# A two-layer decoder trunk on one core: 17 expert weight slots instead of 15, the first step's pieces given back in pairs, and the final norm ahead of the overflow block

## The chip, the cores and the metric

The kernel runs on one core of a Trainium2 chip. The metric is the device time of one execution in microseconds (us). A core has TensorE (PE, with its weight loads as PEld), VectorE (DVE), ScalarE (ACT), GpSimd (POOL) and SyncE (SP); a letter q behind an engine's name means its instruction queue. SP issues all the large weight transfers, one after the other in program order.

## The reference, cut to what matters

Two layers on 256 rows of 1024 numbers, all float32. The first layer ends in a dense SwiGLU, the second in a choice of two of eight experts per row; the last part, from which most of the time comes, is this:

```python
def moe_swiglu(x, w_router, w_gu, w_down):
    logits = jnp.einsum('bsd,de->bse', x, w_router).astype(jnp.float32)
    top_logits, top_idx = lax.top_k(logits, TOP_K)
    top_gates = jax.nn.softmax(top_logits, axis=-1)
    gates = jnp.sum(jax.nn.one_hot(top_idx, N_EXPERTS, dtype=jnp.float32) * top_gates[..., None], axis=-2)
    ...
    for e in range(N_EXPERTS):
        out = out + gates[..., e:e + 1] * swiglu(x, w_gu[e], w_down[e])
    return out

def reference(...):
    ...
            ffn = moe_swiglu(x, w_router[layer // 2], w_gu_moe[layer // 2], w_down_moe[layer // 2])
        x = layer_norm(DEEPNORM_ALPHA * x + ffn, ln2_g[layer], ln2_b[layer])
```

An expert is a SwiGLU with 2816 hidden numbers: 1024 x 5632 weights up and 2816 x 1024 down, so eight experts have 277 MB of weights, and each weight is used once.

## The kernel before, in words

**Order of the work.** Each engine follows its own list of instructions in program order; nothing is chosen at run time except by branches. Up to about 480 us the dense part runs, in which weights are split into a high and a low part (`hi`, `lo`), so that three products make up one float32 product. From then on the experts run, with the raw float32 weights.

**The stream of weights.** Class `Stream` keeps a list of weight pieces of at most 1 MiB (0.75 MiB where a chunk has six column groups), in the order in which they will be used. A piece needs a raw slot. `load` asks SP for the next pieces for as long as a slot is free; `high` and `low` split a dense piece; `done` says that a split piece is used up, and `whole` and `passed` take an expert piece raw and give its slot back. Where `passed` stands in the program, the request of the piece that takes the slot stands too, behind a wait for the products that read the old one. At most eight requests are in the air.

The raw slots of the experts are 15: three that the dense part has already (`RAW = 3`), four in the memory that the attention leaves (`RAW2 = 4`, tag `raw2`), one and one in the memory of the experts (`raw3` and `MORE = 1`, tag `raw5`), and six in the place of the split pieces, three `hi` and three `lo` (`SPLIT = 3`). The last eight of these are opened together, when the dense part's memory is closed.

**Steps.** An expert's 22 column groups (of 128) are cut into chunks of 8, 8 and 6, for the first expert 2, 8, 8 and 4. `STEPS` lists (expert, chunk). A step multiplies the up pieces of its chunk (`up`), then the down pieces of the step before (`down`). There are eight up pieces and three or four down pieces in a full step. At most 64 rows of an expert are handled there; if it has more, which a branch decides (`more_than_half`), `up_more` and `down_more` do the rows 65 to 96 as well, with the same pieces. For more than 96 rows a whole second round exists, in blocks of their own, behind a branch (L1230); here no expert has that many, and the blocks are skipped. The order of the experts 2 to 7 comes from their row counts, which the kernel works out itself: `load_counts` (L969 to L974) loads nine counts into a register on every engine, and six expert numbers on SP.

**Gathers.** Before an expert's first step its rows are gathered by products with a one-hot matrix, `gather`, eight for a batch of experts, each into a PSUM bank (tag `pb`, four banks, of which `down` holds two). `BATCHES` says which experts share one; a batch is made during the expert ahead of its first, as tasks that `some(3)` and `some(2)` spread behind each step's up and down. `turn_hot` turns the one-hots for the way back, `rows_split` splits the expert's output into `yh` and `yl`, and `scatter` adds it to the rows.

**The end.** After the last expert come its `rows_split` and `scatter`, the two branches over the overflow blocks, then the norm of the rows (statistics at L322) and six output transfers (L1242).

Of the kernel before, what the change touches and what calls it, by code (L numbers as in the profile page):

```python
# [20 lines left out]
P = 128  # L21
D = 1024
# [23 lines left out]
def trunk_kernel(ctx: ExitStack, tc: tile.TileContext, x, mem, positions, w_in_a, conv_a, w_q_b,  # L46
# [20 lines left out]
    class Stream:  # L67
# [4 lines left out]
        def __init__(self):  # L72
            self.specs, self.parts, self.raw = [], {}, {}
            self.pools, self.split_pools, self.home = [], [], {}
# [22 lines left out]
        def load(self, limit=None):  # L97
            while self.n_dma < min(len(self.specs), limit or len(self.specs)):
# [8 lines left out]
                raw = p[0].tile([P, PC], F32, name="raw", tag=p[1], bufs=p[2])  # L107
# [14 lines left out]
        def high(self):  # L122
# [4 lines left out]
            hi = p[0].tile([P, PC], F32R, name="hi", tag="hi" + p[1], bufs=p[2])  # L127
# [76 lines left out]
    RAW, RAW2, MORE, SPLIT = 3, 4, 1, 3  # L204
# [125 lines left out]
    def ln_apply(dst, sl, mean, z, gb):  # L330
        nc.vector.scalar_tensor_tensor(dst[:, sl], dst[:, sl], mean, gb[:, 0, sl], op0=OP.subtract, op1=OP.mult)
        nc.vector.scalar_tensor_tensor(dst[:, sl], dst[:, sl], z, gb[:, 1, sl], op0=OP.mult, op1=OP.add)

    def ln_apply_gpsimd(dst, sl, mean, z, gb):
        nc.gpsimd.tensor_scalar(dst[:, sl], dst[:, sl], mean, z, op0=OP.subtract, op1=OP.mult)  # L335
# [512 lines left out]
    def turn_rows(tb):  # L848
        xf[tb] = early.tile([P, KT, P], F32, name="xf", tag="y", bufs=3)
# [22 lines left out]
    st.slots(ring, "hi", SPLIT)  # L872
    st.slots(ring, "lo", SPLIT)
# [15 lines left out]
    g4, e4 = [moe.tile(T4, F32, name=n, tag="sT", bufs=5) for n in ("r_g4", "r_e4")]  # L889
    cnti = moe.tile([P, 2 * NE + 1], I32, name="r_cnti")  # L890
    counts = []
# [31 lines left out]
    def first_hidden(tb, pt):  # L923
# [3 lines left out]
        hd[tb] = moe.tile([P, 2, 256], F32R, name="hd", tag="hd", bufs=2)  # L927
# [51 lines left out]
    BATCHES = ((0, 1), (2, 3, 4), (5, 6, 7))  # L979

    def experts(part):
# [24 lines left out]
        def turn_hot(e):  # L1006
# [3 lines left out]
            turned[e] = moe.tile([P, TB, P], F32R, name="sT", tag="sT", bufs=5)  # L1010
            nc.scalar.copy(turned[e][:CAP].rearrange("p t s -> p (t s)"), ps[:CAP, :TB * P])

        def batch_tasks(es):
            made = []
            return ([lambda: made.extend(one_hots(es))] + [lambda k=k: gather(*made, k) for k in range(KT)] +
                    [lambda e=e: turn_hot(e) for e in es])
# [5 lines left out]
        def up(e, c):  # L1022
# [108 lines left out]
        def first_step(gathers):  # L1131
# [17 lines left out]
            for t in gathers[1:1 + KT]:  # L1149
                t()  # L1150
# [108 lines left out]
```

## Time and profile before

| what | value |
|---|---|
| median of the runs shown | 1182.9 us (1180.91 to 1183.71) |
| the profiled execution | 1181.65 us |
| its span, first to last instruction | 1180.0 us |
| PE busy | 1082.5 us, 92% |
| DVE, ACT, POOL busy | 385.1, 257.7, 62.5 us |
| mean granted clock of PE | 0.976 |
| bytes moved | 353.85 MB |

A busy share is an average over stages with different limits; the dense part (to 480 us) and the experts' part behind it have to be read apart. The page cuts the span into 40 slices of 29.5 us.

### The profile page before, as it was taken

What the parts mean: (1) busy time and instruction counts of PE and PEld (TensorE: products, weight loads), DVE (VectorE), ACT (ScalarE), POOL (GpSimd) and SP (SyncE); (2) the same over time, 40 slices, a digit from 0 to 9 for tenths busy, and PEclk for the clock granted to TensorE, in tenths of its full rate; (3) what the DMA queues carried; (4) which work ended last, traced back from release to release, by engine and by line L of the source; (5) the groups of instructions that cost most, each with busy time, mean ns of one, the idle gap of its engine ahead of it and who ended that gap; (6) DMA issues with size and microseconds to landing.
All of it is one profiled execution on the core that took longest, in us unless ns stands there. A gap on an engine that the chain in (4) does not pass through costs nothing. (4 is left out here: it accounts for less than half of the span.)

```text
span 1180.0 us, 16954 instructions
## 1 busy us (share of the span) xinstructions
PE 1082.5 (92%) x6926; PEld 636.9 (54%) x6926; DVE 385.1 (33%) x595; ACT 257.7 (22%) x367; POOL 62.5 (5%) x47
## 2 busy tenths in 40 slices
PE   8999999999899889897888999999899999999981
PEld 7987899999787656442332343343342343343320
DVE  4767656454776557200110100110210100200105
ACT  5543443443345431110100100100110100100100
POOL 1002000000210220000000000000000000000001
PEclk9999899999989889999999999999999999999995
DMA  9647555556343226699999999999999999999982
GB/s 332 219 165 237 192 178 183 191 165 212 101 149 124 91 72 254 269 401 410 408 403 410 408 404 409 407 389 386 391 388 409 407 405 409 399 391 402 406 343 77
DMA packets 127595, 353.85 MB, mean 300 GB/s; under 512 B 6375, under 2 KB 41968, under 8 KB 127488
## 3 DMA queue, kind: packets, MB, share of 16 engines
q1 hardware_dynamic: 127392, 352.35, 78.7%
q8 instruction: 71, 1.16, 0.4%
q14 instruction: 36, 0.29, 0.1%
q0 software_dynamic: 96, 0.04, 0.0%
HBM read 351.32 MB, written 1.05 MB: 299 GB/s over the span
## 5 line engine op out<-in xcount | busy, mean ns | idle before, releaser
L65 PE MATMUL pa<-raw,xg 128*64 128x512 f32 (+4 forms) x2304 | 388.3, 556 | 21.0 <-DMA raw<-in_w_gu_moe_dram 18.0
L65 PEld LDWEIGHTS pa<-raw,xg 128*64 128x64 f32 (+1 forms) x2304 | 134.2, 128 | 263.8 <-issue 209.6
L65 PE MATMUL pb<-raw,hT 128*64 128x512 f32 x704 | 158.6, 597 | 9.4 <-DMA raw<-in_w_down_moe_dram 3.9
L128 ACT CAST hi<-raw 128x2048 fp32r<-128x2048 f32 (+2 forms) x68 | 124.7, 1836 | 138.7 <-PE pa L65 96.8
L1037 DVE TENSOR_TENSOR h<-h,pa 128x512 f32<-128x512 f32 (+2 forms) x24 | 15.3, 638 | 413.8 <-PE pa L65 401.7
L65 PE MATMUL pa<-xh,hi 128*128 128x256 f32 x528 | 149.7, 284 | 0.2 <-ACT xh L213 0.2
L65 PE MATMUL pa<-xl,hi 128*128 128x256 f32 x528 | 148.5, 281 | 0.3 <-DVE xl L214 0.3
L65 PE MATMUL pa<-xh,lo 128*128 128x256 f32 x528 | 148.5, 281 | 0.0
L138 DVE TENSOR_TENSOR lo<-raw,hi 128x2048 fp32r<-128x2048 f32 (+2 forms) x60 | 130.5, 2182 | 48.1 <-ACT hi L128 48.1
L65 PEld LDWEIGHTS pb<-raw,hT 128*64 128x64 f32 x704 | 48.5, 136 | 106.6 <-issue 88.0
L1036 ACT ACTIVATE h<-pa 128x512 f32<-128x512 f32 (+2 forms) x24 | 13.4, 557 | 416.3 <-PE pa L65 416.3
L65 PEld LDWEIGHTS pa<-xh,hi 128*128 128x128 f32 x528 | 100.0, 189 | 1.6 <-issue 0.8
L65 PEld LDWEIGHTS pa<-xl,hi 128*128 128x128 f32 x528 | 100.0, 189 | 0.9 <-DVE xl L214 0.5
L65 PEld LDWEIGHTS pa<-xh,lo 128*128 128x128 f32 x528 | 99.9, 189 | 0.1
L138 POOL TENSOR_TENSOR lo<-raw,hi 128x2048 fp32r<-128x2048 f32 x8 | 37.7, 4726 | 371.9 <-ACT hi L128 268.9
L65 PE MATMUL pb<-raw,hTx 128*32 128x256 f32 x704 | 40.3, 380 | 3.9 <-DVE hTx L1071 3.9
L1180 POOL MEMSET ya<- 32x1024 f32 x8 | 7.6, 945 | 622.3 <-DVE yl L214 611.8
L65 PE MATMUL pa<-hi,xh 128*128 128x512 f32 (+1 forms) x96 | 36.6, 381 | 0.0
L65 PEld LDWEIGHTS pb<-raw,hTx 128*32 128x32 f32 x704 | 22.5, 110 | 21.4 <-DVE hTx L1071 4.4
L65 PE MATMUL pa<-lo,xh 128*128 128x512 f32 (+1 forms) x96 | 33.9, 354 | 0.0
L1053 DVE TENSOR_TENSOR hx<-hx,pa 64x512 f32<-64x512 f32 (+1 forms) x12 | 7.8, 647 | 78.8 <-ACT hx L1052 78.8
L65 PE MATMUL pa<-hi,xl 128*128 128x512 f32 (+1 forms) x96 | 32.7, 346 | 0.0
(237 smaller groups left out, 1030.6 us busy)
## 6 DMA issues: line engine op xcount, KB each, us to landing
raw<-in_w_gu_moe_dram SPq DMA_DIRECT2D x128, 1024.0 KB, 17.9
raw<-in_w_down_moe_dram SPq DMA_DIRECT2D x88, 1024.0 KB, 17.9
raw<-in_w_gu_moe_dram SPq DMA_DIRECT2D x56, 768.0 KB, 14.7
raw<-in_w_gu_dense_dram SPq DMA_DIRECT2D x44, 512.0 KB, 4.9
raw<-in_w_down_dense_dram SPq DMA_DIRECT2D x11, 1024.0 KB, 4.9
raw<-in_w_in_a_dram SPq DMA_DIRECT2D x8, 1024.0 KB, 9.7
raw<-in_w_o_dram SPq DMA_DIRECT2D x8, 1024.0 KB, 4.9
raw<-in_w_kv_shared_dram SPq DMA_DIRECT2D x6, 1024.0 KB, 5.1
```

The source lines that it names most:

```text
L65: nc.tensor.matmul(o, l, r, start=start, stop=stop, skip_group_check=True)
L128: nc.scalar.copy(hi[:, :n], raw[:, :n])
L138: (nc.gpsimd if self.spare > 0 else nc.vector).tensor_sub(v, raw[:, :n].rearrange("p (a b) -> p a b", a=hi.shape[1]), hi)
L1036: nc.scalar.activation(h[:, :w], pg[:, :w], AF.Silu)
L1037: nc.vector.tensor_tensor(h[:, :w], h[:, :w], pu[:, :w], op=OP.mult)
L1053: nc.vector.tensor_tensor(h[64:, :w], h[64:, :w], px[64:, :w], op=OP.mult)
L1180: nc.gpsimd.memset(down.ya[HALF:CAP], 0.0)
```

## The change

It has four parts. The raw slots become 17: `raw2` has five and `raw5` two, and the six places of `hi` and `lo` are no longer opened together, but each pair when its split piece is used up for the last time (`done`, `turned`). In the first full step, (0,1), the eight up pieces are multiplied and given back in four pairs (`groups`), each with its own branch for the rows over 64. Counts are loaded one batch at a time, and only the first ahead of the first step; batches have two experts each, four batches instead of three; `rows_split` and `down_more` split straight out of PSUM into `yh` and `yl`, without the tile `ya`. The norm and the output (`finish`) stand ahead of the overflow branch, and a second time at the end of the block inside it; the second round is nested in the first, and the output goes through a tile of its own.

```diff
         def slots(self, pool, tag, bufs):
-            self.pools.append([pool, tag, bufs, 0])
+            self.pools.append([pool, tag, bufs, 0, bufs])
             return self.pools[-1]
 
         def split_slots(self, pool, tag, bufs):
             self.split_pools.append([pool, tag, bufs, 0, bufs])
+            self.turned[tag] = [[pool, t + tag, 0, 0, bufs] for t in ("hi", "lo")]
             return self.split_pools[-1]
...
         def done(self):
-            self.home.pop(self.n_done)[3] -= 1
+            p = self.home.pop(self.n_done)
+            p[3] -= 1
             self.n_done += 1
+            if p[2] and self.n_hi == self.n_split:
+
+                p[2] -= 1
+                for t in self.turned[p[1]]:
+                    if t not in self.pools:
+                        self.pools.append(t)
+                    t[2] += 1
+                self.load()
             self.pump()
...
-    RAW, RAW2, MORE, SPLIT = 3, 4, 1, 3
+    RAW, RAW2, MORE, SPLIT = 3, 5, 2, 3
...
     raw3 = st.slots(moe, "raw3", 1)
     st.slots(moe, "raw5", MORE)
-    st.slots(ring, "hi", SPLIT)
-    st.slots(ring, "lo", SPLIT)
     st.load()
...
-    def load_counts():
-        for e in [*range(NE), 2 * NE]:
-            counts.append(nc.values_load(cnti[0:1, e:e + 1], min_val=0, max_val=S))
+    def load_count(e):
+
+        if e not in counts:
+            at = e if e < NE else 2 * NE
+            counts[e] = nc.values_load(cnti[0:1, at:at + 1], min_val=0, max_val=S)
...
     acc = x3
-    BATCHES = ((0, 1), (2, 3, 4), (5, 6, 7))
...
+        def groups(e, c):
+
+            n = len(expert_up(e, c))
+            return [2] * (n // 2) if part == 0 and (e, c) == STEPS[1] else [n]
+
+        def up(e, c, n):
...
             w = CH[e][c][1] * 64
-            g, (pg, pu) = xg[e], banks(2)
-            pcs, k = [], 0
-            while k < KT:
+            if up.k == 0:
+                up.to = banks(2)
+            g, (pg, pu) = xg[e], up.to
+            pcs = []
+            for _ in range(n):
...
+            if up.k == KT:
+                up.k = 0
+                h = moe.tile([P, 512], F32, name="h", tag="h", bufs=2)
+                nc.scalar.activation(h[:, :w], pg[:, :w], AF.Silu)
+                nc.vector.tensor_tensor(h[:, :w], h[:, :w], pu[:, :w], op=OP.mult)
+                hs[e, c] = h
             return pcs
 
-        def up_more(e, c, pcs):
+        up.k = 0
...
             if c == len(CH[e]) - 1:
+                yh, yl = ys[e]
                 for q in range(4):
-                    nc.vector.tensor_copy(down.ya[HALF:CAP, 256 * q:256 * q + 256],
-                                          down.yx[32 * q:32 * q + 32, :256])
+                    sl = slice(256 * q, 256 * q + 256)
+                    split(yh[HALF:CAP, sl], yl[HALF:CAP, sl], down.yx[32 * q:32 * q + 32, :256])
...
         def rows_split(e):
-            ya = down.ya
-            yh, yl = [early.tile([P, D], F32R, name=n, tag="y", bufs=3) for n in ("yh", "yl")]
+            yh, yl = ys[e]
             for q in range(2):
-                nc.scalar.copy(ya[:HALF, 512 * q:512 * q + 512], down.y[64 * q:64 * q + 64])
-            split(yh[:CAP], yl[:CAP], ya[:CAP])
-            ys[e] = yh, yl
+                sl = slice(512 * q, 512 * q + 512)
+                split(yh[:HALF, sl], yl[:HALF, sl], down.y[64 * q:64 * q + 64])
...
+            if pc_ == len(CH[pe_]) - 1:
+                ys[pe_] = [early.tile([P, D], F32R, name=n, tag="y", bufs=2) for n in ("yh", "yl")]
+                for t in ys[pe_]:
+                    nc.gpsimd.memset(t[HALF:CAP].bitcast(F32), 0.0)
...
-            pcs = up(e, c)
-            some(3)
-            hxs[e, c] = moe.tile([P, 512], F32, name="hx", tag="hx", bufs=2)
-            if i > 0:
-                turn_both(prev, prev[0] == e, lambda: up_more(e, c, pcs))
-            else:
-                with more_than_half(e):
-                    up_more(e, c, pcs)
-            for _ in pcs:
-                st.passed()
+            (up_more.to,) = banks(1)
+            for g, n in enumerate(groups(e, c)):
+                k = up.k
+                pcs = up(e, c, n)
+                if g == 0:
+                    some(3)
+                    hxs[e, c] = moe.tile([P, 512], F32, name="hx", tag="hx", bufs=2)
+                if g == 0 and i > 0:
+                    turn_both(prev, prev[0] == e, lambda: up_more(e, c, pcs, k))
+                else:
+                    with more_than_half(e):
+                        up_more(e, c, pcs, k)
+                for _ in pcs:
+                    st.passed()
...
+    def finish():
+
+        y = moe.tile([P, TB, D], F32, name="y_out", tag="raw5", bufs=MORE)
...
+        z = ln_scale(mv, TB)
+        for tb in range(TB):
+            for f, sl in ((ln_apply_gpsimd, slice(896, D)), (ln_apply, slice(0, 448)), (ln_apply, slice(448, 896))):
+                f(y[:, tb], sl, mv[:, tb, 0:1], z[:, tb:tb + 1], gb, acc[:, tb])
+                nc.sync.dma_start(out[0, tb * P:(tb + 1) * P, sl], y[:, tb, sl])
+
     experts(0)
     st.drop(raw3)
     gb = ln_vectors(moe, ln2_g[1], ln2_b[1], tag="raw3")
-    for part in range(1, PARTS):
-        with tc.If(counts[NE] > CAP * part):
+    finish()
+
+    with tc.If(counts[NE] > CAP):
+        expert_specs()
+        st.load()
+        experts(1)
+        with tc.If(counts[NE] > 2 * CAP):
             expert_specs()
             st.load()
-            experts(part)
-
-    mv = small.tile([P, TB, 2], F32, name="ln_mv2")
-    for tb in range(TB):
-        nc.vector.bn_aggr(mv[:, tb], ln_sums(acc[:, tb], None, None))
-    z = ln_scale(mv, TB)
-    for tb in range(TB):
-        for f, sl in ((ln_apply_gpsimd, slice(896, D)), (ln_apply, slice(0, 448)), (ln_apply, slice(448, 896))):
-            f(acc[:, tb], sl, mv[:, tb, 0:1], z[:, tb:tb + 1], gb)
-            nc.sync.dma_start(out[0, tb * P:(tb + 1) * P, sl], acc[:, tb, sl])
```

Three places in the order of instructions are of interest.

The first is SP's list where the experts' stage begins, from the branch of step (0,1) on (L1169 before; L1194 and L1241 after). The DMA rows are the requests for the next pieces, where x2 or x4 counts them. Before:

```order
L1169 COMPARE_AND_BRANCH
L1169 UNCONDITIONAL_BRANCH x2
L109 DMA raw<-in_w_gu_moe_dram 128x2x1024 x2
L115 DMA raw<-in_w_down_moe_dram 128x2x1024 x4
L113 DMA raw<-in_w_gu_moe_dram 128x2x512 x4
L1181 COMPARE_AND_BRANCH
```

and with the change:

```order
L1194 COMPARE_AND_BRANCH
L1194 UNCONDITIONAL_BRANCH x2
L116 DMA raw<-in_w_down_moe_dram 128x2x1024 x2
L1241 COMPARE_AND_BRANCH
L1241 UNCONDITIONAL_BRANCH x2
L116 DMA raw<-in_w_down_moe_dram 128x2x1024 x2
L1241 COMPARE_AND_BRANCH
L1241 UNCONDITIONAL_BRANCH x2
L114 DMA raw<-in_w_gu_moe_dram 128x2x512 x4
L1241 COMPARE_AND_BRANCH
L1241 UNCONDITIONAL_BRANCH x2
L114 DMA raw<-in_w_gu_moe_dram 128x2x512 x4
```

The requests that stood in one block behind one branch now stand in four groups of two or four, each behind a branch of its own.

The second is TensorE's list in the first chunk of expert 3. `pa<-raw,xg 64x512` are the up products, `pb<-so,xth` and `pb<-so,xtl` the gathers, 32x512 the products of `up_more`, L1169 and L1181 (after: L1194 and L1208) the branches. Before:

```order
L65 MATMUL pa<-raw,xg 64x512 x32
L1061 MATMUL pb<-identf,h 128x128 x3
L1169 COMPARE_AND_BRANCH
L65 MATMUL pa<-raw,xg 32x512 x32
L1169 UNCONDITIONAL_BRANCH x2
L1181 COMPARE_AND_BRANCH
L1070 MATMUL pb<-identf,hx 128x64 x3
L65 MATMUL pb<-raw,hTx 32x256 x24
L1181 UNCONDITIONAL_BRANCH x2
L65 MATMUL pb<-raw,hT 64x512 x12
```

and with the change:

```order
L65 MATMUL pa<-raw,xg 64x512 x32
L65 MATMUL pb<-so,xth 128x192 x2
L65 MATMUL pb<-so,xtl 128x192 x2
L65 MATMUL pb<-so,xth 128x192 x2
L65 MATMUL pb<-so,xtl 128x192 x2
L1086 MATMUL pb<-identf,h 128x128 x3
L1194 COMPARE_AND_BRANCH
L65 MATMUL pa<-raw,xg 32x512 x32
L1194 UNCONDITIONAL_BRANCH x2
L1208 COMPARE_AND_BRANCH
L1095 MATMUL pb<-identf,hx 128x64 x3
L65 MATMUL pb<-raw,hTx 32x256 x24
```

Two gathers, each of two pairs of products, are now between the up products and the turns of `h`; the others of the batch follow behind the branches in the same manner. Before, expert 3 had none, and expert 4 had all those for experts 5, 6 and 7.

The third is SP's list at the end, from the last short branch on; `ln_gb` is the norm's scale and offset, L1230 and L1274 the branches over the overflow block. Before:

```order
L1181 COMPARE_AND_BRANCH
L1181 UNCONDITIONAL_BRANCH x2
L312 DMA ln_gb<-in_ln_g_dram 128x1024
L312 DMA ln_gb<-in_ln_b_dram 128x1024
L1230 COMPARE_AND_BRANCH
L113 DMA raw<-in_w_gu_moe_dram 128x4x256 x4
L109 DMA raw<-in_w_gu_moe_dram 128x2x1024 x8
```

and with the change:

```order
L1208 COMPARE_AND_BRANCH
L1208 UNCONDITIONAL_BRANCH x2
L322 DMA ln_gb<-in_ln_g_dram 128x1024
L322 DMA ln_gb<-in_ln_b_dram 128x1024
L1267 DMA out_dram<-y_out 128x128
L1267 DMA out_dram<-y_out 128x448 x2
L1267 DMA out_dram<-y_out 128x128
L1267 DMA out_dram<-y_out 128x448 x2
L1274 COMPARE_AND_BRANCH
L114 DMA raw<-in_w_gu_moe_dram 128x4x256 x4
```

The output transfers, which stood behind both branches, now stand ahead of the one that is left; what follows the branch is the overflow block's own.

## Rows read from the trace of the kernel before

**Rows 1.** The page, part 2: bytes moved per slice of 29.5 us.

```profile
GB/s 332 219 165 237 192 178 183 191 165 212 101 149 124 91 72 254 269 401 410 408 403 410 408 404 409 407 389 386 391 388 409 407 405 409 399 391 402 406 343 77
```

**Rows 2.** Windows: four stretches (columns: us, five engines busy, PEclk, DMA share, GB/s).

```profile
425.00:445.00 20.00, 20.00 (x109) 14.61 (x108) 7.70 (x25) 6.55 (x26) 0.00 (x0) 0.97 0.01 3
490.00:499.00 9.00, 8.18 (x46) 3.82 (x44) 1.26 (x4) 2.08 (x5) 0.00 (x0) 1.00 0.01 5
765.00:775.00 10.00, 10.00 (x96) 4.40 (x98) 3.00 (x5) 1.06 (x2) 0.00 (x0) 1.00 0.93 349
1055.00:1065.00 10.00, 10.00 (x134) 4.81 (x134) 1.54 (x3) 1.56 (x3) 0.00 (x0) 1.00 0.95 344
```

**Rows 3.** Timeline of SP: two requests for expert pieces (start, duration).

```profile
475.79 0.54 SPq L109 DMA_DIRECT2D raw<-in_w_gu_moe_dram  x1
...
497.78 0.57 SPq L109 DMA_DIRECT2D raw<-in_w_gu_moe_dram  x1
```

**Rows 4.** Timeline of PE: start, duration, tile, idle before it and its releaser.

```profile
437.96 0.62 PE L65 MATMUL pa<-hi,ml 128*128 128x512 f32 x2
...
475.20 0.77 PE L65 MATMUL pb<-so,xth 128*128 128x192 f32 x2
482.22 13.95 PE L65 MATMUL pa<-raw,xg 128*64 128x512 f32 x64 [2.91 <-issue]
...
498.48 1.94 PE L65 MATMUL pb<-raw,hT 128*64 128x512 f32 x8 [0.82 <-DVE r_mx L931]
```

**Rows 5.** Line L971, TensorE's queue: ns min/median/max, first to last start.

```profile
L971 PEldq TENSOR_LOAD <-r_cnti x9: 300/308/493, 478.4 to 481.9; - x9
```

**Rows 6.** Windows: four stretches of the experts' stage, columns as in 2.

```profile
540.90:673.00 132.10, 112.68 (x549) 38.72 (x550) 11.83 (x22) 12.51 (x23) 1.89 (x2) 1.00 1.03 407
673.00:888.00 215.00, 208.04 (x1471) 83.45 (x1471) 26.52 (x50) 18.09 (x33) 1.89 (x2) 1.00 1.01 397
933.00:1120.00 187.00, 184.16 (x1335) 71.48 (x1335) 23.62 (x40) 14.41 (x24) 1.89 (x2) 1.00 1.02 402
1120.00:1150.00 30.00, 25.58 (x129) 8.48 (x125) 0.55 (x1) 1.56 (x4) 0.00 (x0) 1.00 0.89 350
```

**Rows 7.** Waits of PE in 540.9:673, 888:933 and 1120:1150 (total, times, longest).

```profile
PE pa L65 <- DMA raw<-in_w_gu_moe_dram: 15.2, 26, 0.8
PE pa L65 <- DMA raw<-in_w_gu_moe_dram: 2.3, 4, 0.6
PE pb L65 <- DMA raw<-in_w_down_moe_dram: 2.3, 4, 0.9
```

**Rows 8.** Timeline of PE: two of the eight gathers for three experts.

```profile
827.88 0.85 PE L65 MATMUL pb<-so,xth 128*128 128x288 f32 x2 [1.49 <-DVE so L990]
...
835.90 0.53 PE L65 MATMUL pb<-so,xth 128*128 128x288 f32 x2 [1.19 <-DVE ya L1084]
```

**Rows 9.** Timeline of ACT and of DVE behind the last expert.

```profile
1149.99 1.17 ACT L1102 COPY ya<-pb 64x512 f32<-64x512 f32 x2 [6.90 <-PE pb L65]
...
1152.32 1.22 DVE L214 TENSOR_TENSOR yl<-ya,yh 96x1024 fp32r<-96x1024 f32 x1 [20.26 <-ACT yh L213]
1154.43 3.31 DVE L1111 SCALAR_TENSOR_TENSOR xt<-pb,r_gates,xt 128x512 f32<-128x512 f32 x4 [0.89 <-PE pb L65]
1164.00 1.29 DVE L322 BATCH_NORM_STATS2 ln_st<-xt 128x6 f32<-128x512 f32 x2 [6.26 <-DVEq L1230]
```

**Rows 10.** Line L1230, the branches over the overflow blocks, columns as in 5.

```profile
L1230 SPq EVENT_SEMAPHORE  x16: 17/17/17, 1155.7 to 1159.4; - x16
L1230 SPq COMPARE_BRANCH  x2: 45/48/50, 1150.9 to 1156.3; - x2
L1230 PEldq COMPARE_BRANCH  x2: 3862/4390/4917, 1153.6 to 1157.7; - x2
```

**Rows 11.** Line L1255, the program's end, columns as in 5.

```profile
L1255 SPq EVENT_SEMAPHORE  x12: 17/28/28, 1176.9 to 1179.9; - x12
L1255 SPq DRAIN  x3: 7/7/13, 1179.0 to 1179.4; - x3
```

More of the change, by code (lines that the diff above doesn't have):

```diff
@@ L106, in load @@
                 n = int(np.prod(dims))
-                raw = p[0].tile([P, PC], F32, name="raw", tag=p[1], bufs=p[2])
+                raw = p[0].tile([P, PC], F32, name="raw", tag=p[1], bufs=p[4])
                 if len(dims) == 3 and dims[0] == 1:
@@ L126, in high @@
             self.home[self.n_hi] = p
-            hi = p[0].tile([P, PC], F32R, name="hi", tag="hi" + p[1], bufs=p[2])
+            hi = p[0].tile([P, PC], F32R, name="hi", tag="hi" + p[1], bufs=p[4])
             nc.scalar.copy(hi[:, :n], raw[:, :n])
@@ L848, in turn_rows @@
     def turn_rows(tb):
-        xf[tb] = early.tile([P, KT, P], F32, name="xf", tag="y", bufs=3)
+        xf[tb] = early.tile([P, KT, P], F32, name="xf", tag="y", bufs=2)
         for h in range(2):
@@ L888, in trunk_kernel @@
     moved, best = rt("r_moved", [P, TB + 2, NF_]), rt("r_best", [P, TB + 2])
-    g4, e4 = [moe.tile(T4, F32, name=n, tag="sT", bufs=5) for n in ("r_g4", "r_e4")]
+    g4, e4 = [moe.tile(T4, F32, name=n, tag="sT", bufs=4) for n in ("r_g4", "r_e4")]
     cnti = moe.tile([P, 2 * NE + 1], I32, name="r_cnti")
-    counts = []
+    counts = {}
     def row_parts(tb):
@@ L1009, in turn_hot @@
                 nc.tensor.transpose(ps[:CAP, tb * P:(tb + 1) * P], oneh[e][:, tb].bitcast(F32), identf)
-            turned[e] = moe.tile([P, TB, P], F32R, name="sT", tag="sT", bufs=5)
+            turned[e] = moe.tile([P, TB, P], F32R, name="sT", tag="sT", bufs=4)
             nc.scalar.copy(turned[e][:CAP].rearrange("p t s -> p (t s)"), ps[:CAP, :TB * P])
@@ L1031, in up, with up_more @@
                         o = q % 2 * 64
[L1032 to L1041 removed]
+                        mm((pu if q > 1 else pg)[o:o + 64, :w], g[:, up.k, :HALF],
+                           pcs[-1][:, i, q * w:(q + 1) * w], start=(up.k == 0))
+                    up.k += 1
+            if up.k == KT:
[4 more added lines that the diff above has]
+                hs[e, c] = h
+            return pcs
+        up.k = 0
+        def up_more(e, c, pcs, k):
             w = CH[e][c][1] * 64
[L1043 to L1044 removed]
+            g, px = xg[e], up_more.to
             for piece in pcs:
@@ L1150, in first_step @@
                 t()
+            load_orders()
             first_hidden(1, pt[1])
[L1152 removed]
+            load_count(0)
         def first_acc():
@@ L1178, in down_both @@
                 down.y, down.yx = bank(), bank()
-                down.ya = early.tile([P, D], F32, name="ya", tag="y", bufs=3)
-                nc.gpsimd.memset(down.ya[HALF:CAP], 0.0)
+            if pc_ == len(CH[pe_]) - 1:
+                ys[pe_] = [early.tile([P, D], F32R, name=n, tag="y", bufs=2) for n in ("yh", "yl")]
+                for t in ys[pe_]:
+                    nc.gpsimd.memset(t[HALF:CAP].bitcast(F32), 0.0)
             with more_than_half(pe_):
@@ L1224, in experts @@
             t()
+    def finish():
+        y = moe.tile([P, TB, D], F32, name="y_out", tag="raw5", bufs=MORE)
+        mv = small.tile([P, TB, 2], F32, name="ln_mv2", tag="ln_mv2", bufs=1)
+        for tb in range(TB):
+            nc.vector.bn_aggr(mv[:, tb], ln_sums(acc[:, tb], None, None))
+        z = ln_scale(mv, TB)
+        for tb in range(TB):
+            for f, sl in ((ln_apply_gpsimd, slice(896, D)), (ln_apply, slice(0, 448)), (ln_apply, slice(448, 896))):
+                f(y[:, tb], sl, mv[:, tb, 0:1], z[:, tb:tb + 1], gb, acc[:, tb])
+                nc.sync.dma_start(out[0, tb * P:(tb + 1) * P, sl], y[:, tb, sl])
     experts(0)
```

38 lines of the change are left out of this document (17 added, 21 removed).

## The prediction

> **What bounds the kernel now.** I read the profile from coarse to fine: the page's slices, windows of the experts' stage, the waits of TensorE in each of those windows, and single rows where the change touches.
>
> The slices [rows 1] show 400 to 410 GB/s from about 500 us to the end, with small dips, and 72 to 270 GB/s in the four slices before. So from 500 us on the weight stream is close to its rate, while ahead of it there is a hole. The hole has pieces [rows 2]: 425 to 445 us moves 3 GB/s and 490 to 499 moves 5. The second one is plain in SyncE's rows [rows 3]: 17 pieces are asked for by 475.79, the next only at 497.78. By then step (0,1) has used up its eight pieces, which the kernel gives back all at once.
>
> From the stream's rate, 407 GB/s [rows 6], a 1 MiB piece costs 1.049 MB / 407 GB/s = 2.58 us.
>
> TensorE by stretch [rows 6]: experts 1 and 2 up to 673 us, busy 112.7 of 132.1, and it waits 15.2 us for up weights [rows 7]: bound by the stream. 673 to 888, 208.0 of 215 busy, and the waits show no DMA: bound by TensorE. Around 888 to 933 the waits name the stream again (2.3 us), 933 to 1120 not at all, and 1120 to 1150 is idle 4.4 us, 2.3 of it waiting for the last down weights [rows 6, 7]. The order of the experts is decided by their row counts; those with more than 64 rows cost TensorE more than the stream, the others less. So the end is set by turns, and time given to one side counts only until the other takes over. This is why I add up along the experts, not over the span.
>
> **The stream's lead.** Before, at 516 us the stream has delivered 17 pieces + (516 - 499.1)/2.58 = 23.5 pieces.
>
> After: two slots are at hand that before waited for later memory, and the slots of the three last split pieces are turned into stream slots as soon as those are multiplied. The first is used up at 438.6 us (the row of 437.96 is its last product [rows 4]). So the stream restarts near 440, five to six us ahead of 445, and it has 17 slots to fill. Two of them come back at 471 to 476 as before (475.79 [rows 3]). TensorE then loads one register instead of nine: nine cost 479.31 to 482.22, the 2.91 us of idle ahead of up(0,1) [rows 4, 5], so it starts near 479.6. Its pieces come back in pairs, 13.95/4 = 3.5 us apart plus a skip each. From row 498.48 two short skips cost 0.82 us together [rows 4], so I take 0.4 each: three more are 1.2 us. The pairs come at 483.5, 487.4, 491.3 and 495.2, each worth 5.2 us of stream, so the stream runs on: three of the 17 were there before 440, the other 14 and the two given back last to 440 + 16 x 2.58 = 481, a pause of some 2 us follows, and then the pairs come faster than it uses them up. 17 + 2 + 8 + 1 (the piece of down(0,0)) = 28 pieces, all there by 481 + 2 + 9 x 2.58 = 507; the next slot comes only when up(0,2) ends, 498.5 + 2 + 14 = 514. Lead at 516: 28 - 23.5 = 4.5 pieces, **11.4 us**. TensorE's stream waits up to 673 (15.8 us with the down weights [rows 7]) are enough to turn all of it into an earlier expert 3.
>
> **The batches.** Batches of two make a fourth one-hot stage. Before, the last three experts are gathered together at expert 4 (light, but bound by TensorE there). After, (4,5) is done in expert 3 and (6,7) in expert 5, both heavy. Price of a 192-wide gather: eight take 475.20 to 479.31, so 0.51 each [rows 4]. For a batch of two: 8 x 0.51 = 4.1, two turns of 0.3, two or three register loads of 0.3, and the waits of the kind the wide gathers met, 1.49 for the one-hots and 1.19 for a bank, once each [rows 8]: 7 to 8, taken as **+7** in experts 3 and 5. The three-expert batch: 8 x 0.8 (the 288-wide products in rows 8 run 1.5 times as wide), three turns, and the same two waits: **-10** at expert 4.
> Along the path: expert 2 -11.4; expert 3 -4.4; expert 4 wants -14.4, but the stream bounds it at -11.4, for TensorE waited for it there already (2.3 us at 888 to 933); expert 5 back to -4.4. At the end the stream is still 11.4 ahead, so the idle of 1120 to 1150 goes: between 2.3 (the wait) and 4.4 (all of it), taken as 3.6. **TensorE ends 8.0 earlier.** Bounds: -11.4 + 7 - 10 + 7 - 4.4 = -11.8 if the stream gives way at expert 4, and -4.4 if the end idle stays.
>
> **The tail** [rows 9]. TensorE's last product is done at 1149.99, where two copies into ya start; one cast of 96x1024 and one subtraction follow, and the first add starts at 1154.43, 4.44 later. After, each half is cast from PSUM (0.58, half of the 1.17 for two copies) and subtracted (half of 1.22 = 0.61); the two halves overlap by one step, and 0.9 goes for the product ahead of the add: 0.58 + 0.61 + 0.9 = 2.1. **-2.3** (from -1.5, if reading PSUM makes the subtraction slower, to -2.6). The norm's first statistics stand 6.26 behind the adds, released by VectorE's two far skips over the overflow blocks [rows 9]; after, no branch is ahead of them: **-6.2**. One skip then lies behind the last output DMA on SyncE. Before, two took 1150.9 to 1159.4 there, unseen: 5.4 and 3.1 us with their events [rows 10]. Behind the last output DMA 1176.9 to 1179.0 is spent waiting for it to land [rows 11]; with 3.1 to 5.4 in place of 2.1 the end is 1.0 to 3.3 later, **+2.2**. Separate y_out tiles, the copies of down_more that turn into casts, the memsets on GpSimd: at nothing, behind TensorE's 208 busy of 215; without that cover the eight casts and subtractions of a heavy expert would cost some 4 us once each.
>
> Sum: 1181.65 (the profiled execution; 0.1% under the median 1182.9, its span 1180.0) - 8.0 - 2.3 - 6.2 + 2.2 = **1167.4**; from the median it would be 1168.6. I say 1168.
>
> **Rivals.**
> A, all lead kept: 17 slots also remove the dips (six windows from 765 to 1065 like the two in rows 2, worth (1 - 349/408) x 10 and so on, 7.8 us together), and the gathers hide behind waits. TensorE -11.4 - 7.8 = -19, tail -6.3: **1156**. For it: the stream runs 4.5 pieces ahead where it was behind. Against: 673 to 888 is bound by TensorE [rows 6], which the dips only mirror.
> D, the lead is two pieces only: early slots are filled sooner but the stream then stops, full, before the first pair comes back. 2 x 2.58 = 5.2: expert 2 -5.2, expert 3 +1.8, expert 4 and 5 -5.2 to +1.8, end idle -2.7: TensorE -0.9, tail -6.3: **1174.5**. Against: the 16 pieces from 440 last to 481, and the first pair comes at 483.5.
> B, each new skip costs TensorE what a far one does, 3.9 to 4.9 us [rows 10], three of them 13 us: the lead is spent at step (0,1), expert 3 to 5 end at +1.8 + 7 - 10 + 7 = +5.8, less the end idle, +2.5; tail -6.3: **1178**. Against: the short skips of row 498.48, 0.82 for two.
> The Trainium skill (Runtime: NRT & Kernel Launch, section Instruction fetch mechanics) says that a taken branch whose target lies outside the two pages of instructions at hand forces a fetch before the engine goes on. By that rule a skip over eight matmuls waits for nothing and one over an overflow block does; the trace agrees, 0.82 us for two short ones against 3.9 to 4.9 for a far one [rows 4, 10]. By the short price the sum is 1167.4, by the far price B's 1178.
> C, slower: every gather inside experts 3 and 5 waits for a PSUM bank, as one did for 1.19 us [rows 8], since down holds two of the four banks and the adds and turns want the others: 16 x 1.19 = 19 us, at experts that TensorE bounds: 1167.4 + 19 = **1186**. It decides from 0.9 us a gather. For it: the heavy experts have more bank users. Against: of the eight wide gathers one waited for a bank.
> That the stream changes nothing at all would still leave the tail, 1175.
>
> **Chances.** Forecast 0.55 (1161 to 1173 by its bounds), A 0.17, D 0.13, B 0.08, C 0.07. 0.2% (2.4 us) is about what a measurement can tell here from no change. Faster: forecast, A, D and half of B, 0.88, less a little for mishaps not listed: 0.86; within: 0.07; slower: C, 0.07. The range leaves out C, a part of A and a part of B: 1156 to 1178.
>
> **What would show it.** The stream busy from 440 to 507 with a pause of no more than some 3 us; 28 pieces by 514; up(0,1) starting near 479.6 and lasting 15 us; TensorE's waits for the stream before expert 3 down from 16 to about 4 us; gathers in experts 3 and 5 worth 7 us each, none at expert 4; last product near 1142; first add 2.1 us behind it; no branch ahead of the statistics; 4 to 6 us between the last output DMA and the end. I am wrong if the stream stops for long between 481 and 499, if the short skips show more than 1 us, if gathers wait for banks, or if the stream falls behind in experts 4 to 7, so that the lead is not there to remove the end idle.

## The result and the profile after

The changed kernel takes 1166.21 us (median; 1165.85 to 1166.54), the kernel before in the same comparison 1181.91 (1180.26 to 1183.71): a ratio of 0.9867, 95% interval 0.985 to 0.9884. Forecast were 1168 us and a range of 1156 to 1178. The profiled execution has a span of 1164.7 us.

The page after, part 2, bytes moved per slice (29.1 us each):

```profile
GB/s 330 215 178 221 210 186 181 175 187 195 95 153 131 86 103 382 351 329 408 406 406 408 407 406 409 400 328 398 391 404 409 406 406 408 406 345 401 407 404 81
```

Against [rows 1], the slices from 437 to 495 us rise from 254 and 269 to 382 and 351, and two dips are deeper than any between 501 and 1121 us before (386): 328 in the slice from 757 us on and 345 in the one from 1019, in experts 3 and 6.

The windows after, columns as in [rows 2]:

```profile
480.00:490.00 10.00, 9.55 (x50) 3.91 (x47) 0.23 (x1) 0.88 (x3) 0.00 (x0) 1.00 0.69 254
499.10:516.00 16.90, 15.63 (x76) 6.07 (x74) 3.84 (x15) 3.85 (x5) 0.00 (x0) 1.00 0.74 274
540.90:673.00 132.10, 119.55 (x675) 48.02 (x673) 15.37 (x28) 11.01 (x22) 3.67 (x4) 0.99 1.03 407
673.00:888.00 215.00, 205.54 (x1372) 81.35 (x1370) 22.63 (x44) 17.14 (x36) 3.67 (x4) 0.99 0.99 392
933.00:1120.00 187.00, 183.76 (x1314) 72.11 (x1308) 23.70 (x41) 15.37 (x31) 5.51 (x6) 1.00 1.00 396
```

The hole at 490 to 499 us of [rows 2] is gone. What is left of it are two short ones: 480 to 490 loses (1 - 254/408) x 10 = 3.8 us, and 499 to 516 loses 5.5. Both are in the prediction's sum, as a pause of 2 us behind 481 and as one from 507 to 514. In the second the slots are full until up(0,2) is done, and SyncE asks for the next pieces from 511.2 on.

TensorE's waits for the stream, in 540.9 to 673 and in 888 to 933 us (total, times, longest), against 15.2 and 2.3 in [rows 7]; none is left between 1120 us and the last product:

```profile
PE pa L65 <- DMA raw<-in_w_gu_moe_dram: 8.0, 12, 2.1
...
PE pa L65 <- DMA raw<-in_w_gu_moe_dram: 0.6, 1, 0.6
```

TensorE's rows where the experts' stage begins, for [rows 4]:

```profile
477.06 3.65 PE L65 MATMUL pa<-raw,xg 128*64 128x512 f32 x16
480.65 1.09 PE L65 MATMUL pb<-so,hd 128*128 128x96 f32 x8
481.58 0.62 PE L1023 MATMUL pb<-identf,so 128*96 128x128 f32 x4
482.35 7.46 PE L65 MATMUL pa<-raw,xg 128*64 128x512 f32 x32
489.96 3.65 PE L65 MATMUL pa<-raw,xg 128*64 128x512 f32 x16
494.86 1.94 PE L65 MATMUL pb<-raw,hT 128*64 128x512 f32 x8 [1.25 <-DVEq L1241]
496.60 13.93 PE L65 MATMUL pa<-raw,xg 128*64 128x512 f32 x64
510.46 0.66 PE L1086 MATMUL pb<-identf,h 128*128 128x128 f32 x4
```

The 2.91 us of register loads are gone: up(0,1) follows the gathers without a gap. The price of a short skip has to be read from start to start, since a row goes on while the next product already runs (496.60 + 13.93 is 510.53, and the next row starts at 510.46). The 64 products of up(0,2), without a skip among them, take 510.46 - 496.60 = 13.86 us, so 32 take 6.93. The 32 from 482.35 on, with one skip among them and one behind them, take 489.96 - 482.35 = 7.61. That is 0.34 us for each skip, near the 0.4 of the prediction.

The gains along the experts are best read from one instruction that stands once in each step: VectorE's product of the two halves of an up result (`h<-h,pa`, L1037 before, L1060 after; called the h rows below; the first row of the table is its like in the dense part, L926 and L936). Here (3,1) is the second step of expert 3. Experts 2, 3, 5 and 6 are the heavy ones, with more than 64 rows; the others are light. Its start times, and the end of TensorE's last down product (us):

| place | before | after | after - before |
|---|---|---|---|
| expert 0, first hidden rows (dense part) | 465.70 | 463.52 | -2.2 |
| (0,1) | 496.28 | 493.73 | -2.6 |
| (1,0) | 560.86 | 549.09 | -11.8 |
| (2,0) | 644.52 | 628.91 | -15.6 |
| (3,0) | 734.01 | 718.79 | -15.2 |
| (3,1) | 765.15 | 758.54 | -6.6 |
| (4,0) | 826.51 | 821.44 | -5.1 |
| (5,0) | 904.55 | 891.72 | -12.8 |
| (5,1) | 932.65 | 924.74 | -7.9 |
| (6,1) | 1025.15 | 1020.54 | -4.6 |
| (7,2) | 1131.51 | 1126.01 | -5.5 |
| last down product | 1149.95 | 1140.78 | -9.2 |
| span | 1180.0 | 1164.7 | -15.3 |

The first row is ahead of every instruction of TensorE that the change moves. In the other profiles below it lies between 462.99 and 465.44, the lowest in a kernel whose dense part is the old one; so 2.2 us of this pair belong to the execution and not to the change. Most of it goes with TensorE's granted clock. From 124.5 to 125.2 us this was 0.50 (1.2 GHz) in the profile before and in six of the others, and there the first row stands at 465.23 to 465.70. In the profile after and in the other six it was 1.00 again by then, and the row stands at 462.99 to 464.26.

Behind the last expert, ACT and DVE, for [rows 9]:

```profile
1140.87 0.58 ACT L223 CAST yh<-pb 64x512 fp32r<-64x512 f32 x1 [5.51 <-PE pb L65]
1142.28 0.58 ACT L223 CAST yh<-pb 64x512 fp32r<-64x512 f32 x1 [0.83 <-DVE yl L224]
...
1143.62 2.73 DVE L1135 SCALAR_TENSOR_TENSOR xt<-pb,r_gates,xt 128x512 f32<-128x512 f32 x4
1146.26 1.28 DVE L332 BATCH_NORM_STATS2 ln_st<-xt 128x6 f32<-128x512 f32 x2
```

The statistics follow the adds at once. The first add stands 2.75 us behind the first cast, where it stood 4.44 behind the first copy: the second half's cast waits for the first half's subtraction, so the halves do not overlap. And SyncE's end, the branch behind the output transfers, for [rows 10]:

```profile
L1274 SPq EVENT_SEMAPHORE  x8: 17/17/17, 1162.6 to 1163.1; - x8
...
L1274 SPq COMPARE_BRANCH  x1: 45/45/45, 1159.4 to 1159.4; - x1
```

Its skip takes 1159.4 to 1162.6, 3.2 us, its events 0.5, and 1.6 later is the end.

### The profile page after: what moved, and what is told of

It is laid out like the page before. It is cut to its first block, busy times and chain, and to the rows that moved or that the text cites. A ratio compares the mean times of both kernels' runs of the same rounds, so it can differ in the third digit from the quotient of the medians.

```text
span 1164.7 us, 17138 instructions
## 1 busy us (share of the span) xinstructions
PE 1082.7 (93%) x6958; PEld 643.8 (55%) x6958; DVE 386.6 (33%) x607; ACT 256.0 (22%) x379; POOL 69.8 (6%) x55
## 5 line engine op out<-in xcount | busy, mean ns | idle before, releaser
L65 PEld LDWEIGHTS pa<-raw,xg 128*64 128x64 f32 (+1 forms) x2304 | 140.3, 129 | 245.8 <-issue 212.4
L1060 DVE TENSOR_TENSOR h<-h,pa 128x512 f32<-128x512 f32 (+2 forms) x24 | 15.3, 637 | 400.3 <-PE pa L65 388.8
L1207 POOL MEMSET yh<- 32x1024 f32 x8 | 7.6, 944 | 626.9 <-PE pb L65 617.5
L224 DVE TENSOR_TENSOR yl<-pb,yh 64x512 fp32r<-64x512 f32 (+1 forms) x32 | 17.7, 555 | 69.0 <-ACT yh L223 69.0
## 6 DMA issues: line engine op xcount, KB each, us to landing
raw<-in_w_gu_moe_dram SPq DMA_DIRECT2D x56, 768.0 KB, 15.7
```

Source lines behind the costliest of these rows:

```text
L65: nc.tensor.matmul(o, l, r, start=start, stop=stop, skip_group_check=True)
L224: nc.vector.tensor_sub(lo, src, hi)
L1060: nc.vector.tensor_tensor(h[:, :w], h[:, :w], pu[:, :w], op=OP.mult)
L1207: nc.gpsimd.memset(t[HALF:CAP].bitcast(F32), 0.0)
```

## The experiments

The theory after the result: the lead of the stream at 516 us is what TensorE gains up to expert 2; from there on TensorE is the bound, so gathers in heavy experts take part of it back; the end gains because no branch stands ahead of the norm any more. The rivals are told with each run. No run takes back the loads of the counts or the splits straight out of PSUM alone, so what these are worth is not shown. Ratios are to the kernel before, run in the same comparison; the changed kernel has 0.9867.

**The pairs.** All eight pieces of step (0,1) given back at once:

```diff
-            return [2] * (n // 2) if part == 0 and (e, c) == STEPS[1] else [n]
+            return [n]
```

> The changed kernel with the eight up pieces of step (0,1) given back all at once. Theory (the stream's lead is what TensorE gains, and from expert 3 on TensorE is the bound): the stream, which is full near 481 us, restarts only near 493, after up(0,1); it loses about 12 us there instead of 2, and gains back some 2 us because it is not full again before up(0,2) ends. TensorE waits about 8 us more for up weights before 673 us and everything behind it is that much later: +6 to +9, 1172 to 1175 us. Rival (a lead is given back later anyway, as it shrank from 15 us at expert 2 to 5 at expert 7): TensorE is later at expert 2 and not at the end, +0 to +2.

1172.37 us, ratio 0.9923 (0.991 to 0.9937): 6.2 above the changed kernel, the theory's value. The first window is where it is lost; the second shows that the stream is not full again before 516. Windows of this run:

```profile
480.00:499.00 19.00, 17.87 (x90) 6.95 (x88) 0.91 (x2) 1.48 (x4) 0.23 (x1) 1.00 0.27 98
499.00:516.00 17.00, 15.73 (x76) 6.06 (x74) 3.83 (x15) 3.85 (x5) 0.00 (x0) 1.00 1.04 396
```

**The early places.** The hi and lo places opened together with the experts' memory, 17 slots kept:

```diff
-            if p[2] and self.n_hi == self.n_split:
+            if False:
...
     st.slots(moe, "raw5", MORE)
+    st.slots(ring, "hi", SPLIT)
+    st.slots(ring, "lo", SPLIT)
```

> The changed kernel, 17 slots, but the six places of split pieces are opened together with the experts' memory, as before the change. Theory: the stream restarts near 444.5 instead of 439, stops near 457 for 5 us, then runs on without the two pauses of 2 us each near 482 and 507: 5 us less lead, +4 to +6, 1170 to 1172 us. Rival (the early places only fill slots that would be full in time): the pauses take it all, +0 to +1.

1167.28 us, ratio 0.9879 (0.9864 to 0.9894): 1.1 more than the changed kernel, a difference that these intervals do not tell from none. The theory's 4 to 6 did not come. The rival is right, and the windows say why: the stream starts later, but then has neither of the two holes. What it is late it would have stood full.

```profile
480.00:499.00 19.00, 17.30 (x86) 6.67 (x84) 1.34 (x3) 1.69 (x5) 1.83 (x2) 1.00 1.03 409
499.00:516.00 17.00, 15.73 (x76) 6.18 (x74) 2.83 (x14) 3.85 (x5) 0.00 (x0) 1.00 1.04 394
```

**The number of slots.** 15 and 16, everything else as in the changed kernel:

```diff
-    RAW, RAW2, MORE, SPLIT = 3, 5, 2, 3
+    RAW, RAW2, MORE, SPLIT = 3, 4, 1, 3
```

(for 16: 3, 4, 2, 3).

> The changed kernel with 15 slots (four and one in place of five and two). Theory: two pieces less in the lead at 516 us, 5 us, and the stream stops more often later, since it can run ahead of TensorE by two pieces less: +5 to +8, 1171 to 1174 us. Rival (15 are enough once the early places and the pairs are there): +0 to +2.

> The changed kernel with 16 slots (four and two). Theory (each slot is 2.6 us that the stream can run on while TensorE is slower than it, in expert 3 and again in expert 6, and 2.6 us of lead): half of what the two slots cost together, +6 to +9, 1172 to 1175 us. Rival (the loss begins only below a certain number, where expert 4 starves): +0 to +3.

With 15 it takes 1181.3 us, ratio 1.0002 (0.9992 to 1.0013): all of the gain is gone, though pairs, early places and tail are there. With 16 it takes 1174.0, ratio 0.9935 (0.9919 to 0.9951). So a slot is worth 7 to 8 us here, each of the two about the same, where I had counted one piece of stream time, 2.6. For 15 my number was too small by half; for 16, with that known, it held. The windows of the kernel with 15 slots, experts 3 and 4:

```profile
760.00:888.00 128.00, 122.83 (x818) 48.70 (x812) 14.86 (x26) 10.64 (x22) 3.67 (x4) 1.00 0.93 360
888.00:933.00 45.00, 38.60 (x211) 12.70 (x209) 4.18 (x10) 3.46 (x7) 0.00 (x0) 1.00 1.03 409
```

From 760 to 888 the stream moves 360 GB/s (389 with 17 slots, 374 with 16, and 390 in the kernel before, whose expert 3 has no gathers, in the same window): its slots are full while TensorE works at a heavy expert with gathers. Then, at the light expert 4, the stream cannot make up for it: it runs at its full 409, and TensorE is busy only 38.6 of 45 us, against 42.3 with 17 slots. The wait in the second window has grown from 0.6 to 4.3:

```profile
PE pa L65 <- DMA raw<-in_w_gu_moe_dram: 4.3, 7, 0.6
```

And behind 1120 us TensorE waits for the last down weights, as in the kernel before and not in the changed one:

```profile
PE pb L65 <- DMA raw<-in_w_down_moe_dram: 2.8, 4, 1.3
```

This profile is of the slowest of the run's eleven executions (1184.89).

**The batches alone.** The kernel before with nothing but the four batches of two:

```diff
-    BATCHES = ((0, 1), (2, 3, 4), (5, 6, 7))
+    BATCHES = ((0, 1), (2, 3), (4, 5), (6, 7))
```

> The kernel before, with nothing changed but the batches: (0,1), (2,3), (4,5), (6,7). Theory (gathers inside expert 3 hold TensorE back by 8 to 10 us there, the full slots then stop the stream, and expert 4, which needs the stream, cannot make up for it with 15 slots): TensorE 10 later behind expert 3, back to some +5 at expert 4, where it waits for weights, and +8 more at expert 5: +8 to +15, 1189 to 1196 us. Rival (what expert 3 pays, expert 4 saves): +0 to +3.

1193.72 us, ratio 1.0102 (1.0083 to 1.012): slower by 11 to 12 us, as the theory has it. Its profile is of the fastest of six executions (1188.16). By the h rows it is 2.7 ahead of the kernel before up to (3,0) (the whole of it already there in the dense part), 2.5 behind at (3,1), 5.6 behind at (4,0), even at (4,1), 0.8 ahead at (4,2), and 2.5, 5.7 and 8.8 behind at (5,0), (5,1) and (6,0). Expert 3 takes 8.4 us; expert 4, without gathers, saves 6.5 and then loses 3.3 again, waiting for the stream; expert 5 takes another 6.4.

**15 slots with the old batches.** The rest of the change, so to speak: pairs, early places, straight splits and tail, with 15 slots and three batches. Not shown in the cut are the buffers that three experts in a batch need, four in place of two for `y` and five in place of four for `sT`; so the batches of two also free memory.

```diff
-    RAW, RAW2, MORE, SPLIT = 3, 5, 2, 3
+    RAW, RAW2, MORE, SPLIT = 3, 4, 1, 3
...
-    BATCHES = ((0, 1), (2, 3), (4, 5), (6, 7))
+    BATCHES = ((0, 1), (2, 3, 4), (5, 6, 7))
```

> The changed kernel with 15 slots (four and one) and the old three batches (and the yh, yl and turned one-hots in as many buffers as these need). Theory (the two extra slots pay above all for the gathers that the batches of two put into the heavy experts): without both, the lead of some 8 us at expert 2 lasts to the end, as the stream's stops follow TensorE, and the tail gives 6: 1168 to 1171 us. Rival (15 slots cannot hold the lead in any case): the tail's gain and little more, 1175 to 1178 us.

1174.39 us, ratio 0.9949 (0.9929 to 0.997), between the two; its seven executions lie from 1172.38 to 1179.17, the widest here. The lead of 10 us is whole at (4,0) (-9.4), and then falls to -6.1 at (4,1), -5.2 at (5,0) and -2.9 at (5,1). So 15 slots hold it through the heavy experts 2 and 3 and lose most of it at expert 4 with its gathers. Batches of two and two more slots together are worth some 8 us to the change. Without the slots the batches of two cost 11 in the kernel before and 7 in the changed one (1181.3 against 1174.39). 17 slots with three batches were not run.

**The norm.** The changed kernel with `finish()` behind the two overflow branches:

```diff
-    finish()
-
-    with tc.If(counts[NE] > CAP):
...
-        with tc.If(counts[NE] > 2 * CAP):
...
-        finish()
+    for part in range(1, PARTS):
+        with tc.If(counts[NE] > CAP * part):
+            expert_specs()
+            st.load()
+            experts(part)
+    finish()
```

> The changed kernel with the norm and the output behind the two overflow branches again. Theory: the statistics stand 6 us behind the last add, and the last transfers end 2 us sooner: +4 (3.5 to 5), 1170 us. Rival (VectorE would have had to wait for something else there, the norm's vectors or GpSimd): +0 to +1.

1169.74 us, ratio 0.9897 (0.9882 to 0.9912): 3.5 more than the changed kernel, the lower end of the theory.

**A wait that the batches made.** In expert 3 the profile after shows a gather that stands and what follows it:

```profile
730.61 2.80 PE L65 MATMUL pb<-raw,hTx 128*32 128x256 f32 x48 [1.50 <-DVE hTx L1096]
733.34 0.47 PE L65 MATMUL pb<-so,xth 128*128 128x192 f32 x2
...
737.02 0.47 PE L65 MATMUL pb<-so,xth 128*128 128x192 f32 x2 [2.99 <-DVE yl L224]
...
737.64 7.07 PE L65 MATMUL pb<-raw,hT 128*64 128x512 f32 x24
```

The second of these gathers waits 2.99 us for a bank until the last of expert 2's four splits is done; and the 24 down products behind it take 7.07 us, where the same took 5.37 in the kernel before. Their windows in the profile after (PEclk is the last column but two):

```profile
739.00:741.00 2.00, 2.00 (x6) 0.49 (x4) 0.00 (x0) 0.00 (x0) 0.00 (x0) 0.50 1.04 412
743.00:745.00 2.00, 2.00 (x12) 0.61 (x10) 0.00 (x0) 0.19 (x1) 0.00 (x0) 1.00 1.03 410
```

TensorE ran at half its clock, 1.2 GHz, from 739 to 741, after it had stood for 3 us; at 743 it is at 2.4 again. So the wait cost 3.0 + 1.7. This is no chance of one execution: in all six profiles that have this wait (those of the changed kernel, no pairs, late slots, 15 and 16 slots, norm behind) the clock falls to half in it or right behind it, and in none of the five below without it does it fall there. A second stretch at half clock in the profile after has no such wait ahead of it: at 896 to 900 the granted clock is 0.73, and 64 products of expert 5 take 8.77 us and not 7.07, behind waits of 0.62, 0.60 and 1.31. Here the tasks of an expert's last step are put behind its down products:

```diff
-            some(2)
+            if pc_ < len(CH[pe_]) - 1:
+                some(2)
             down(pe_, pc_, pcs)
+            if pc_ == len(CH[pe_]) - 1:
+                some(2)
```

> The changed kernel, in which the two tasks of an expert's last down step stand behind its down products and not ahead of them. Theory: the gather that waits 3.0 us for VectorE's last split in expert 3 finds its bank free, since 5.4 us of down products lie between, and from expert 3 on TensorE is the bound: -2.5 to -3, 1163.5 us. Rival (the wait only moves: the bank is late, or the stream becomes the bound at expert 4): 0 to -1.

1161.34 us, ratio 0.9826 (0.981 to 0.9843): 4.9 less than the changed kernel, more than I had said, since the clock's 1.7 comes on top of the wait's 3.0. By the h rows, less the 1.9 by which the dense parts differ, it is 5.0 ahead at (3,1). Behind that the two executions differ by the clock again, each by one stretch at half clock: this one in expert 4 (0.50 from 822 to 825), the changed kernel's in expert 5. In its trace the gathers follow at once, and the down products take 5.37:

```profile
735.07 5.37 PE L65 MATMUL pb<-raw,hT 128*64 128x512 f32 x24
740.37 0.47 PE L65 MATMUL pb<-so,xth 128*128 128x192 f32 x2
```

With it, the one-hots ahead of the up products:

```diff
-                    tasks += batch_tasks(b)
+                    made = batch_tasks(b)
+                    made[0]()
+                    tasks += [lambda: None] + made[1:]
```

> As the run before, and the one-hots of a batch are made ahead of the step's up products and not behind them, so that the first gather need not wait for VectorE (1.3 us in each of three batches). Theory: 3 x 1.3 = 3.9 less of TensorE's time, of which the one in expert 1 is hidden by the stream: -2.6 beside the -3 of the run before, 1160 to 1161 us. Rival (the stream is the bound again once TensorE is 3 us faster): no more than the run before, 1163.

1158.01 us, ratio 0.9801 (0.9783 to 0.982): 3.3 less again; the theory had 2.6.

**Where the gathers stand.** On top of this, the gathers of (6,7) at the light expert 4 (their turned one-hots still at expert 5):

```diff
-                if e == b[0] - 1 and c == 0:
+                late = b[0] == 6
+                if e == b[0] - 1 - late and c == 0:
                     made = batch_tasks(b)
                     made[0]()
-                    tasks += [lambda: None] + made[1:]
+                    tasks += [lambda: None] + (made[1:1 + KT] if late else made[1:])
+                if late and e == b[0] - 1 and c == 0:
+                    tasks += made[1 + KT:]
```

> The kernel with tasks behind down and one-hots early, with the gathers of (6,7) at expert 4 (64 rows or less) and not at expert 5 (more). Theory: from expert 3 on TensorE is busy in both and the stream waits for it, so that moving 4 us of gathers moves nothing at the end: 0 to -1, 1157 to 1158 us. Rival (an expert that costs TensorE more than the stream must not get gathers, one that costs less can hide them): -3 to -4, 1154 us.

1157.53 us, ratio 0.9788 (0.9774 to 0.9801), beside 0.9801 of the run before: no difference that these intervals show. The total is the theory's, but not for the theory's reason. By the h rows, less the 1.1 by which the dense parts differ, TensorE is 1.5 us later at (5,0), 1.2 earlier at (6,0) and 3.5 earlier from (6,1) to (7,2): the light expert hides most of the gathers, as the rival has it. At the last down product only 1.2 of it is left, because TensorE now waits there for the last weights, for which it does not wait in the run before:

```profile
PE pb L65 <- DMA raw<-in_w_down_moe_dram: 1.5, 3, 0.8
```

So the end is set by the stream here, and a place that is cheaper for TensorE gains little until the stream is ahead too.

**Pairs in two steps.** With the tasks and one-hots of above, step (0,2) gives back in pairs too:

```diff
-            return [2] * (n // 2) if part == 0 and (e, c) == STEPS[1] else [n]
+            return [2] * (n // 2) if part == 0 and (e, c) in STEPS[1:3] else [n]
```

> The kernel with tasks behind down and one-hots early, and step (0,2) too gives its eight up pieces back in pairs. Theory: between 499 and 516 us the stream moves only 274 GB/s, since all slots are full from some 507 until up(0,2) is done and its branch passed at 513; with pairs these 5.5 us are filled, three short skips cost about 1.2, and TensorE still waits 8 us for up weights before 673: -3 to -4, 1154 to 1155 us. Rival (TensorE is the bound behind expert 2 and the lead is given back there): 0 to -1.

1152.42 us, ratio 0.9754 (0.9737 to 0.9772): 5.6 less than without, the fastest of all. The hole of 274 GB/s is filled:

```profile
499.00:516.00 17.00, 15.72 (x74) 5.74 (x72) 0.69 (x1) 2.47 (x3) 0.00 (x0) 1.00 1.04 402
```

The gain is larger than I had said: it is the whole 5.5 us of the hole. The three short skips are there, some 1.0 us by the 0.34 of step (0,1), but they do not show in the total; TensorE waits for up weights behind them anyway, 5.1 us from 540.9 to 673, where that wait was 8.0 without the pairs. And the same kernel with the early places taken away, to see whether they were worthless or only covered (the edit is that of the second experiment):

> The kernel with pairs in the steps (0,1) and (0,2), tasks behind down and one-hots early, but with the six places of split pieces opened together with the experts' memory. Theory (the early places were worth 1 us in the changed kernel only because the stream, ahead of time, then stood full for 5 us between 507 and 513; with pairs in step (0,2) it no longer stands, and the early start is kept): +4 to +6, 1157 to 1158 us. Rival (the early places are worth 1 us in any case): 1153 to 1154 us.

1158.81 us, ratio 0.9808 (0.9794 to 0.9821): 6.4 more. So the early places were covered: worth some 1 us, within the noise, while the stream stood full from 507 to 511 anyway, and 6 once it did not.

## Why the prediction was right, and where it was not

**The stream's lead** was right in its mechanism; its size was off by little. Forecast were 4.5 pieces (at 2.58 us each 11.6, not 11.4). Between 425 and 516 us the stream moves 235 GB/s before and 303 after: (303 - 235) x 91 / 1049 = 5.9 pieces, 15.2 us, of which the early dense part accounts for 2.2; so the change's own lead is 13.0. The step that was off is "the next slot comes only when up(0,2) ends, 498.5 + 2 + 14 = 514": I had shifted up(0,1) to its new time and not up(0,2), whose products end at 510.5, or 512.7 without the early dense part. That is 1.3 us, most of what is missing. The skips were priced right, 0.4 forecast and 0.34 measured, though the 0.82 us of row 498.48 end, by that row, with a wait for VectorE and are not the price of two skips alone. That the lead would all be taken up by expert 3 held: -15.2 at (3,0). But it was not all taken up as waits for the stream: up to (3,0) these fall from 16.8 us to 8.6, and not to about 4 as the prediction's sign said, and 2.9 more are the loads that are gone.

**What made the lead** I had not taken apart: the prediction gives it to early places, slots and pairs together. Undone one at a time, the pairs are worth 6.2 (rival D, a stream that stands until up(0,1) is done, lay 7.1 above the sum), the early places 1.1, within the noise.

**The batches.** "+7 in experts 3 and 5": expert 3 took 10.1 (-15.2 at (3,0) to -5.1 at (4,0)) and expert 5 8.2. The prediction's own items add up to 8.0 to 8.3, not to "7 to 8": 4.1 + 0.6 + two or three loads of 0.3 + 1.49 + 1.19. In expert 3 the bank wait was 2.99 and not 1.19, and the clock's 1.7 came behind it, a term that the prediction does not have. Expert 5 had no bank wait, but the clock's 1.7 at 896 to 900. Rival C named the right place, but one gather met it and not sixteen. The return at expert 4, 7.0 by the sum, was 7.7.

**The slots.** This is the step that failed without showing in the total. The prediction counted the two slots as two pieces of lead; taking them away costs 15.1 us, not 5.2. By the h rows, less the 1.7 by which the two executions differ in the dense part, the kernel with 15 slots is 5.0 behind the changed one at (3,0), which is the two pieces; 6.3 at (4,0), 13.0 at (5,0), 11.3 from (5,1) to (7,2) and 15.3 at the last down product. So the 10 us that I had no term for arise in two places, 6.7 in expert 4 and 4.0 at the end, where TensorE waits for the last weights again; the step from 13.0 to 11.3 is the changed kernel's own clock in expert 5. A slot more lets the stream run on for one more piece beside a heavy expert, and the light expert behind it, and the end, wait that much less. The prediction named this as a way to be wrong ("if the stream falls behind in experts 4 to 7, so that the lead is not there to remove the end idle") but gave the slots no price for it. Rival A had the thought with the wrong sign: the dips do not go, they are deeper (328 and 345 GB/s, in expert 3 and behind the gathers of expert 5), but TensorE hardly waits any more for what they leave out.

**The tail.** First add -1.7 (forecast -2.3: the halves do not overlap); statistics -6.9 (forecast -6.2; 0.6 of it shorter adds: 2.73 for four, not 3.31); behind the last output transfer +2.2 (forecast +2.2), and 0.2 in the norm itself. Sum -6.2 against -6.3. Undoing the norm's move cost 3.5 against 4.0.

**The end idle** was 3.7 (from -5.5 to -9.2), forecast 3.6. The last down product is 9.2 earlier, 7.0 without the execution's 2.2, forecast 8.0.

So the sum of -14.3 came near the measured -15.7, but in part by luck. The parts of this pair of profiles add up to -7.0 - 6.2 = -13.2 without the dense part's 2.2, which no part of the change explains. And within TensorE's 7.0 errors cancel: the lead was 1.6 larger than forecast and expert 4 gave back 0.7 more, while the batches took 4.3 more in experts 3 and 5; another 0.9 came between (6,1) and (7,2). What stays open is why the clock stays at half for longer in the dense part of some executions than of others.

## What to carry to other kernels

A stream that runs beside an engine of changing speed needs slots for the slow stretches, not for the mean: here each of the last two was worth three times its own transfer time, because without it a light expert behind a heavy one starved, and the end too. Parts of such a change don't add up: the batches of two cost 7 to 11 us at 15 slots, and together with the two slots they gain 8; the early places were worth some 1 us until the next hole was closed, then 6. Look for the next time the queue stands full before pricing an earlier start, and put a task whose bank is freed by slow engines behind the products that can cover it. And where work is moved to a cheaper place, look at the end of the path as well as at the place.

## What the runs showed of the hardware

A branch that skips eight matmuls costs TensorE 0.34 us between products (7.61 us for 32 products and two skips, 6.93 for 32 without), a tenth or less of the far skips of [rows 10], 3.9 to 4.9. And a wait of 3 us in the experts' stage costs more than itself: 24 products behind it took 7.07 us instead of 5.37, at a granted clock of 0.50 in 739 to 741, and the clock fell behind this wait in each of the six profiles that have it. But the length of one wait does not tell when this comes. An idle time of 2.91 us ahead of up(0,1) in the kernel before [rows 4] was not followed by it (13.95 us for 64 products, as in other steps), while at 896 to 900 the clock was 0.73 behind waits of no more than 1.31; the runs do not say what the difference is.
